# Three pairs of r tiles and one more gate pair as seven products of quarters, with linear attention's outputs parked in DRAM

## The chip, the cores and the metric

The kernel runs on one core of one Trainium2 chip. Its time is the device time of one execution in microseconds; a kernel's time is the median of its runs. Beside them stands one execution that the hardware profiler recorded. All lines L... are lines of the kernel before.

## What is computed

One decoder layer runs over 560 tokens: 512 prompt tokens, 32 sample tokens (8 sequences of 4) and 16 meta tokens. Two half-step FFNs stand around a mixer with two branches, gated linear attention and stick-breaking attention. The mixer is where the change is:

```python
u = rms_norm(h, mix_pre_g)
proj = u @ w_in                       # q_a, k_a, v_a, gk, r_a, q_b, k_b, v_b, gate_a, gate_b
o_a, s_new = gla_branch(q_a, k_a, v_a, g, s0, lead)
o_a = rms_norm(o_a, gla_norm_g).reshape(B, L, V_GLA) * jax.nn.silu(r_a)
o_b = sb_attend(q_b, keys, vals, sb_bias, q_off)      # keys of sample tokens: cache pages by page_table
m = jax.nn.sigmoid(gate_a) * (o_a @ w_o_gla) + jax.nn.sigmoid(gate_b) * (o_b @ w_o_sb)
h = h + rms_norm(m @ w_out, mix_post_g)
```

All is float32. The model width is 1024, so r_a, gate_a, gate_b, o_a and o_b are 1024 wide each.

## The kernel before

**Layout and products.** Activations lie transposed: 128 features on the partitions, the tokens along the row. A tile of a product is 128 output features by all tokens, over eight blocks of 128 input features. Each float32 operand is split into two float32r parts: `hi`, a cast, and `lo`, the difference. A product is hi·hi + hi·lo + lo·hi, three matmuls. TensorE is PE in the profile, VectorE DVE, ScalarE ACT, GpSimd POOL, SyncE SP.

**Two kinds of tiles.** A plain tile ("R" in the lists, `tile_steps`, L674 to L687) does the eight blocks for two column halves of 280 and 264 tokens: eight steps of six matmuls. A pair of tiles ("S", `seven_steps`, L998 to L1032) takes two weight tiles as a 2 by 2 matrix of quarters and the activations as another, and makes the four result quarters from seven quarter products instead of eight, by Strassen's scheme in Winograd's form. It is 14 steps of six matmuls of 272 columns. It needs sums of weight quarters (`weight_sums`), sums of activation quarters (`usum`, s1 to s4) and sums of products. Its four accumulators a, d, b, c take all four PSUM buffers of the tag `acc`; `copied` and `add` take the products out.

**Steps set the order.** PE, VectorE, ScalarE and GpSimd run in the program's own order. The program counts steps: after each one `step()` runs what `later(n, f)` put n steps ahead, and then what `then` or `when` set for that step. So each engine's queue is written out by hand; an instruction that waits holds up all that stands behind it on its engine. SP, which issues the plain DMAs, is in order too, and runs ahead of the steps as far as its own waits let it.

**Stages.** FFN 1 (16 of its 22 hidden tiles as pairs of gate and up), its down product, the values, then linear attention by four heads (`Head`), whose outputs `oa[head, e]`, eight tiles of 544 tokens, stay in SBUF until the r tiles use them. Meanwhile the sums of quarters of u are made (`whole_u`, `u_sums`) and stored to `sums_dram`. Then eight passes for pairs of stick-breaking heads (`Pair`), 24 steps each: queries, keys and values of this pair, with the attention of the pair before in between. A ninth pass finishes the last pair; its 24 steps are the r tiles 0, 1 and 2 (`gate_r`).

**The mixer's list.** `MIXER` names the tiles that follow: r3 to r7, o0 to o7 (`out_a`, o_a @ w_o_gla), a0 and a1 (`gate_a`), then the pairs b0, a2 and b2 (`gate_pair`), the plain p0 and p1 (o_b @ w_o_sb), and so on. Of the sixteen gate tiles a0 and a1 are plain; the other fourteen are seven pairs, named by their first tile. The sums of u come back at steps 80 to 104 (`SUMS_BACK`) and are split into hi and lo 8 and 10 steps later. A plain r tile is done as follows: ScalarE takes sigmoids from the accumulators, VectorE multiplies by the accumulators and by `oa`, and `split` makes the parts `oas` that the o tiles read.

**Weights.** `st.todo` is the list of weight blocks; three blocks can be in flight (tag `raw`). `st.fetch` issues the next one on SP and waits until its buffer is free. `weights_at` lays out a pair's weight work around its first step n: sums at n - 10 to n - 8, parts b1 at n - 6 and n - 5, t at n - 2 and n - 1, b2 at n and n + 1, t4 at n + 4 and n + 6.

**The sample tokens' cache.** `ask` gathers four pages of keys or values by indirect DMA on the POOL queue (L2069) into rooms from `ring`, a list that each user refills when it is done. `use_keys` turns them (L2118), `sample_products` (L2132) and `sample_values` (L2218) multiply. All this is tied to step numbers of the ninth pass and of the mixer.

**Rooms.** `Arena` holds SBUF tiles: 25 rooms of six units, a unit being 280 columns. A request takes neighbouring units of a room that holds the same type, or of an empty one; among those that fit it takes the one given back longest ago. A writer of a room waits until the last reader of what lay there is done.

Of the kernel before, what the change touches and what calls it, by code (L numbers as in the profile page):

```python
# [1 line left out]

# [47 lines left out]
UNITS = 150  # L50


class Arena:
# [4 lines left out]
    CHUNK = 6  # L58

    def __init__(self, pool, n):  # L60
        self.pool, self.clock, self.made = pool, 0, 0
        self.freed = [[0] * self.CHUNK for _ in range(n // self.CHUNK)]
        self.tile = [None] * len(self.freed)
        self.held = {}
        self.keep = 0

    def take(self, width, dt=F32, tight=False):
# [3 lines left out]
        for c, free in enumerate(self.freed):  # L71
            empty = None not in free
            if not empty and self.tile[c].dtype != dt:
                continue
            for s in range(self.CHUNK - k + 1):
# [6 lines left out]
                key = (empty and empties <= self.keep, waste, tight and sum(x is not None for x in free), alone, since)  # L82
# [4 lines left out]
        if None not in self.freed[c] and (self.tile[c] is None or self.tile[c].dtype != dt):  # L87
            self.made += 1
            self.tile[c] = self.pool.tile([P, self.CHUNK * self.UNIT], dt, tag=f"room{c}", name=f"room{c}_{self.made}")
# [32 lines left out]
def hybrid_step(  # L122
# [15 lines left out]
    arena = Arena(cp, UNITS)  # L138
# [103 lines left out]
    ob_dram = dp.tile([8, P, NP], F32, name="ob_dram")  # L242
    sums_dram = dp.tile([4, 2, P, NP + NS], F32, name="sums_dram")
# [86 lines left out]
    class Head:  # L330
# [246 lines left out]
        def out(self, e):  # L577
# [867 lines left out]
    st.todo += [(win, 0, KD, C_RA + P * n, P, False) for n in range(8)]  # L1445
# [4 lines left out]

    for kind, what, n in MIXER[5:]:
        w, c = {"a": (win, C_GA), "b": (win, C_GB), "o": (w_o_gla[0], 0), "p": (w_o_sb[0], 0)}[what]
# [612 lines left out]
    ring = []  # L2065

    def page(src, i, c):
        t = ring.pop(0)
# [43 lines left out]
    def sample_keys(b, q, kp, kT):  # L2112
# [8 lines left out]
        if q:  # L2121
            ring.extend((kp[b, 0], kp[b, 1]))
# [88 lines left out]
    def sample_values(c, b0, vp, oz):  # L2211
# [8 lines left out]
        ring.extend(vp.values())  # L2220
# [62 lines left out]

    def gate_r(n):

        acc = yield from tile_steps(um, W1)
        sg, o = take(NW), oa[n // 2, n % 2]
# [16 lines left out]
    def gate_a(n):  # L2304
        acc = yield from tile_steps(um, W1)
        sg = take(NW)

        def sig():
            for h in range(2):
                S.activation(sg[:, h * HW : h * HW + W2[h]], acc[h][:, : W2[h]], AF.Sigmoid)  # L2310

        def by():
            tt(m1[n], sg, m1[n], ALU.mult)
# [388 lines left out]
```

## Time and profile before

| | |
|---|---|
| median of 3 runs | 1506.97 us (1506.46 to 1508.04) |
| the profiled execution | 1508.72 us, span 1507.0 us |
| granted clock | 0.999 |
| matmul records | 11941 |
| DMA | 180.40 MB, mean 120 GB/s |
| r tiles 0 to 7 | about 802 to 874 us of the span |
| o tiles | about 874 to 936 us |
| gate and p tiles | about 937 to 1068 us |

A row of a stretch gives, for each engine, its busy time and its number of instructions there, then the granted clock, the busy share of the DMA engines and what they moved. A row of a group of instructions gives line, engine, operation, output and inputs with their shapes, the count, then the busy time in us and the mean duration in ns, and behind the second bar the engine's idle time just before them with what ended it. A row of the timeline gives start and duration in us, and in brackets the idle time of the engine before it. The helper `tt` puts all VectorE operations of two tensors on L153, so those are told apart by tiles and shapes.

### The profile page before, as it was taken

What the parts mean: (1) busy time and instruction counts of PE and PEld (TensorE: products, weight loads), DVE (VectorE), ACT (ScalarE), POOL (GpSimd) and SP (SyncE); (2) the same over time, 40 slices, a digit from 0 to 9 for tenths busy, and PEclk for the clock granted to TensorE, in tenths of its full rate; (3) what the DMA queues carried; (4) which work ended last, traced back from release to release, by engine and by line L of the source; (5) the groups of instructions that cost most, each with busy time, mean ns of one, the idle gap of its engine ahead of it and who ended that gap; (6) DMA issues with size and microseconds to landing.
All of it is one profiled execution on the core that took longest, in us unless ns stands there. A gap on an engine that the chain in (4) does not pass through costs nothing.

```text
span 1507.0 us, 29698 instructions
## 1 busy us (share of the span) xinstructions
PE 1494.2 (99%) x11941; PEld 1442.1 (96%) x11941; DVE 1090.0 (72%) x1939; ACT 771.5 (51%) x1422; POOL 149.3 (10%) x216
## 2 busy tenths in 40 slices
PE   9999999999999999999999999999999999999998
PEld 8999999999999889999888899999999999999998
DVE  5888888853787866877776534977567898888544
ACT  6545454533655556565555343634564555455334
POOL 2000000000000011123324551000000000000000
PEclk9999999999999999999999999999999999999999
DMA  8123333336565473335555568335532233333352
GB/s 250 55 86 99 99 98 97 88 101 195 147 160 148 122 112 85 91 82 118 131 105 139 169 204 192 105 96 144 152 103 79 85 111 99 99 99 89 86 168 98
DMA packets 276458, 180.40 MB, mean 120 GB/s; under 512 B 10154, under 2 KB 260736, under 8 KB 276320
## 3 DMA queue, kind: packets, MB, share of 16 engines
q1 hardware_dynamic: 270864, 161.64, 40.6%
q0 software_dynamic: 5440, 16.85, 3.2%
q8 instruction: 94, 1.54, 0.4%
q14 instruction: 44, 0.36, 0.1%
q10 hardware_dynamic: 16, 0.00, 0.0%
HBM read 155.72 MB, written 22.74 MB: 118 GB/s over the span
## 4 chain that ended last, share of the span: by engine, by line
PE 94%; DVE 2%; DMA 2%; ACT 1%; issue 0%; DVEq 0%; SPq 0%; ACTq 0%
PE acc L682 8%; PE acc L1248 8%; PE acc L1249 8%; PE acc L685 8%; PE acc L683 8%; PE acc L1250 8%; PE acc L695 7%; PE acc L698 7%; PE acc L696 7%; PE acc L1191 2%; PE acc L1188 2%; PE acc L1189 2%; PE acc L1028 1%; PE acc L1029 1%; PE acc L1030 1%; PE ps L2023 1%
## 5 line engine op out<-in xcount | busy, mean ns | idle before, releaser
L153 DVE TENSOR_TENSOR lo<-raw,hi 128x1024 fp32r<-128x1024 f32 (+1 forms) x213 | 254.9, 1197 | 125.9 <-ACT hi L661 102.5
L153 DVE TENSOR_TENSOR room<-room,room 128x544 f32<-128x544 f32 (+17 forms) x413 | 259.0, 649 | 81.4 <-ACT room L740 15.0
L682 PE MATMUL acc<-room,hi 128*128 128x280 f32 (+1 forms) x928 | 271.2, 309 | 0.2 <-DVE room L156 0.2
L1249 PE MATMUL acc<-room,hi 128*128 128x280 f32 (+1 forms) x896 | 259.3, 289 | 0.0
L1248 PE MATMUL acc<-room,hi 128*128 128x280 f32 (+1 forms) x896 | 259.3, 289 | 0.0
L1250 PE MATMUL acc<-room,lo 128*128 128x280 f32 (+1 forms) x896 | 259.1, 289 | 0.0
L683 PE MATMUL acc<-room,hi 128*128 128x280 f32 (+1 forms) x928 | 250.3, 289 | 0.1
L685 PE MATMUL acc<-room,lo 128*128 128x280 f32 (+1 forms) x928 | 192.8, 289 | 0.0
L682 PEld LDWEIGHTS acc<-room,hi 128*128 128x128 f32 x928 | 174.7, 188 | 13.1 <-issue 11.0
L683 PEld LDWEIGHTS acc<-room,hi 128*128 128x128 f32 x928 | 175.0, 189 | 2.8 <-issue 1.9
L1248 PEld LDWEIGHTS acc<-room,hi 128*128 128x128 f32 x896 | 168.6, 188 | 0.0
L1250 PEld LDWEIGHTS acc<-room,lo 128*128 128x128 f32 x896 | 168.6, 188 | 0.0
L1249 PEld LDWEIGHTS acc<-room,hi 128*128 128x128 f32 x896 | 168.4, 188 | 0.0
L959 ACT CAST hi<-raw 128x1024 fp32r<-128x1024 f32 x92 | 96.4, 1052 | 133.1 <-PE acc L1249 48.8
L661 ACT CAST hi<-raw 128x1024 fp32r<-128x1024 f32 (+1 forms) x121 | 122.7, 1015 | 72.0 <-DMA raw<-in_ffn_w_down_dram 18.6
L685 PEld LDWEIGHTS acc<-room,lo 128*128 128x128 f32 x928 | 145.0, 188 | 0.0
L695 PE MATMUL acc<-room,hi 128*128 128x280 f32 (+2 forms) x498 | 143.7, 296 | 0.9 <-ACT hi L661 0.9
L696 PE MATMUL acc<-room,hi 128*128 128x280 f32 (+2 forms) x498 | 141.5, 292 | 0.0
L698 PE MATMUL acc<-room,lo 128*128 128x280 f32 (+2 forms) x498 | 128.4, 292 | 0.7 <-DVE lo L153 0.7
L959 ACT CAST hi<-room 128x1024 fp32r<-128x1024 f32 x84 | 70.2, 836 | 80.8 <-PE acc L1249 60.3
L695 PE MATMUL acc<-room,room 128*128 128x280 f32 (+3 forms) x366 | 107.8, 295 | 0.0
L153 DVE TENSOR_TENSOR lo<-room,hi 128x1024 fp32r<-128x1024 f32 x84 | 80.2, 955 | 36.7 <-ACT hi L959 36.5
(406 smaller groups left out, 3299.5 us busy)
## 6 DMA issues: line engine op xcount, KB each, us to landing
raw<-in_w_in_dram SPq DMA_DIRECT2D x49, 512.0 KB
raw<-in_ffn_w_down_dram SPq DMA_DIRECT2D x40, 448.0 KB
raw<-in_ffn_w_gate_dram SPq DMA_DIRECT2D x64, 256.0 KB
raw<-in_ffn_w_up_dram SPq DMA_DIRECT2D x64, 256.0 KB
out_dram<-room SPq DMA_DIRECT2D x36, 256.0 KB
raw<-in_ffn_w_down_dram SPq DMA_DIRECT2D x14, 512.0 KB
raw<-in_w_in_dram SPq DMA_DIRECT2D x28, 256.0 KB
h_dram<-room SPq DMA_DIRECT2D x24, 280.0 KB
```

The source lines that it names most:

```text
L153: (eng or V).tensor_tensor(out=out, in0=a, in1=b, op=op)
L661: S.copy(h_, src)
L682: T.matmul(acc[h][:, : wid[h]], hi[k], a[h][0], start=(k == 0), stop=False)
L683: T.matmul(acc[h][:, : wid[h]], hi[k], a[h][1], start=False, stop=False)
L685: T.matmul(acc[h][:, : wid[h]], lo[k], a[h][0], start=False, stop=(k == KD - 1))
L695: T.matmul(acc[h][:nw, : wid[h]], wh, a[h][0], start=(k == 0), stop=False)
L696: T.matmul(acc[h][:nw, : wid[h]], wh, a[h][1], start=False, stop=False)
L698: T.matmul(acc[h][:nw, : wid[h]], wl, a[h][0], start=False, stop=(k == kt - 1))
L959: S.copy(hi[:, :kt], src)
L1248: T.matmul(x[:, :QW], hi, act[k][0], start=(first and k == 0), stop=False, skip_group_check=True)
L1249: T.matmul(x[:, :QW], hi, act[k][1], start=False, stop=False, skip_group_check=True)
L1250: T.matmul(x[:, :QW], lo, act[k][0], start=False, stop=(k == 3), skip_group_check=True)
```

## The change

- r2 and r3, r4 and r5, r6 and r7 become three pairs (`r_pair`), a0 and a1 become one (`gate_pair`). `gate_a` goes. The ninth pass now runs the first 24 steps of the mixer's own chain: r0, r1 and eight steps of r2's pair. Step 0 stays at the end of that pass, so r0 has step -24.
- In `r_pair` VectorE makes the four result quarters in two tiles `t`, ScalarE their sigmoids, VectorE multiplies `oa` by both, and `split` follows.
- The sums of u come back at steps -31 to -19 and are split 5 to 8 steps later.
- Each head's two outputs `oa` are stored to `oa_dram` and their rooms given back; `oa_back` reads them again, for a plain tile at its start, for a pair at its sixth step.
- The second column halves of u's first four tiles are given back before r2 (`halved`).
- Pages get a room at each ask instead of one from `ring`, and the asks have a spacing of their own: steps 7, 15, 23, 31, 39, 63, 71, 79 and 87 of the mixer, before 7 to 63 by eights and 87.
- `Arena` has 14 rooms of six units and 33 of two; a request of up to two units takes a short room if any fits.
- The splits of o_b for the p tiles start 6 steps after b0's beginning, before 2.

```diff
-SUMS_BACK = (80, 88, 96, 104)
-MIXER = [("R", "r", n) for n in range(3, 8)]
-MIXER += [("R", "o", n) for n in range(8)] + [("R", "a", 0), ("R", "a", 1), ("S", "b", 0), ("S", "a", 2), ("S", "b", 2), ("R", "p", 0), ("R", "p", 1)]
+SUMS_BACK = (-31, -27, -23, -19)
+MIXER = [("R", "r", 0), ("R", "r", 1), ("S", "r", 2), ("S", "r", 4), ("S", "r", 6)]
+MIXER += [("R", "o", n) for n in range(8)] + [("S", "a", 0), ("S", "b", 0), ("S", "a", 2), ("S", "b", 2), ("R", "p", 0), ("R", "p", 1)]
...
-    CHUNK = 6
+    LONG, SHORT = 6, 2
...
-        self.freed = [[0] * self.CHUNK for _ in range(n // self.CHUNK)]
+        self.freed = [[0] * self.LONG for _ in range(n)] + [[0] * self.SHORT for _ in range((UNITS - n * self.LONG) // self.SHORT)]
...
-                key = (empty and empties <= self.keep, waste, tight and sum(x is not None for x in free), alone, since)
+                key = (k <= self.SHORT < len(free), empty and empties <= self.keep, waste, tight and sum(x is not None for x in free), alone, since)
...
                 give(*self.on)
+                for e in range(2):
+                    later(1, lambda e=e: nc.sync.dma_start(oa_dram[2 * hd + e], oa[hd, e]))
+                    later(6, lambda e=e: give(oa.pop((hd, e))))
...
-        t = ring.pop(0)
+        t = take(512)
...
-        ring.extend(vp.values())
+        give(*vp.values())
...
+    def oa_back(n):
+        o = take(NW)
+        nc.sync.dma_start(o, oa_dram[n])
+        return o
...
     def gate_r(n):
+        o = oa_back(n)
         acc = yield from tile_steps(um, W1)
-        sg, o = take(NW), oa[n // 2, n % 2]
+        sg = take(NW)
...
+    def r_pair(n):
+        o, t, sg, outs = {}, {}, {}, {}
+        q0, q1 = slice(0, QW), slice(QW, NW)
+        def load():
+            for i in range(2):
+                o[i] = oa_back(n + i)
+        def second():
+            t[1] = take(NW)
+            outs.update(c12=t[1][:, q0], c22=t[1][:, q1])
+        def first():
+            t[0] = take(NW)
+            outs.update(c11=lambda a: S.copy(t[0][:, q0], a), c21=t[0][:, q1])
+        def by_t(i):
+            sg[i] = take(NW)
+            S.activation(sg[i], t[i], AF.Sigmoid)
+            tt(o[i], o[i], t[i], ALU.mult)
+        def by_sg(i):
+            tt(o[i], o[i], sg[i], ALU.mult)
+            give(t[i], sg[i])
+            split(oas, n + i, o[i], oap)
+        for d, f in ((6, load), (10, second), (11, first), (14, lambda: by_t(1)), (15, lambda: by_sg(1)), (16, lambda: by_t(0)),
+                     (17, lambda: by_sg(0))):
+            later(d, f)
+        yield from seven_steps(("r", n), usum, QW, outs)
...
-        for k in (i, i + 4):
-            for h in range(2):
+            for h in range(1 if k < 4 else 2):
...
+        starts, n = {}, -24
+        for i in range(4):
+            when(SUMS_BACK[i], sums_back, i)
+            for m in range(2):
+                when(SUMS_BACK[i] + 5 + m, sums_hi, i, m)
+                when(SUMS_BACK[i] + 7 + m, sums_lo, i, m)
...
-            for n in FE:
+            for n in FE if now else ():
...
-            for main in (now.queries, now.keys, now.values) if now else (lambda i=i: gate_r(i) for i in range(3)):
+            for main in (now.queries, now.keys, now.values) if now else (lambda: islice(mixer, 24),):
...
-            when(8 * i + 7, ask)
+        for i in range(3, 12):
+            when(8 * i - 17 if i < 8 else 8 * i - 1, ask)
...
-            when(starts["b", 0] + 2 + 4 * i, lambda i=i: split(obs, i, ob[i], obp))
+            when(starts["b", 0] + 6 + 4 * i, lambda i=i: split(obs, i, ob[i], obp))
```

More of the change, by code (lines that the diff above doesn't have):

```diff
@@ L2121, in sample_keys @@
         if q:
-            ring.extend((kp[b, 0], kp[b, 1]))
+            give(kp[b, 0], kp[b, 1])
     def sample_products(c, b0, q, kT, z):
@@ L2445, in hybrid_step @@
                 then(SUM[1], last.meta_summed)
-            if pr == 4:
-                ring += [take(512) for _ in range(4)]
             if pr > 4:
@@ L2568, in hybrid_step @@
         when(starts["p", 6] + 2, h_back)
[L2569 removed]
         n = 0
[L2571 to L2581 removed]
+        for _ in mixer:
+            n += 1
+            step()
+            for f, args in mixer_at.pop(n, ()):
+                f(*args)
+        assert not mixer_at, sorted(mixer_at)
         hT_room = hT_room_
```

107 lines of the change are left out of this document (48 added, 59 removed).

## The prediction

> **What bounds the kernel now.** First the page: busy time of the engines (part 1) and the chain of waits (part 4).
>
> ```profile
> PE 1494.2 (99%) x11941; PEld 1442.1 (96%) x11941; DVE 1090.0 (72%) x1939; ACT 771.5 (51%) x1422; POOL 149.3 (10%) x216
> ...
> PE 94%; DVE 2%; DMA 2%; ACT 1%; issue 0%; DVEq 0%; SPq 0%; ACTq 0%
> ```
>
> PE is busy 1494.2 of 1507.0 us and makes up 94% of the chain. Whatever takes matmuls away shortens the run, as long as nothing else begins to hold PE up. So the second view is the list of PE's own waits over the whole run, of which the two in the part that changes are these (us in total, times, longest):
>
> ```profile
> PE ps L2218 <- issue: 2.7, 5, 0.8
> ...
> PE acc L1028 <- DVE room L153: 0.3, 1, 0.3
> ```
>
> The 2.7 us lie in the sample-value matmuls and wait for nothing that the profile shows; the 0.3 us are a quarter-product tile waiting for VectorE. Third, busy time by stretch: the first four r tiles with the rest of the last attention pair, the other four r tiles, the three gate pairs that run back to back, and a piece of the second FFN, which is all seven-product tiles.
>
> ```profile
> core 0: us, PE busy (x) PEld busy (x) DVE busy (x) ACT busy (x) POOL busy (x), PEclk, DMA share, GB/s
> 802.00:839.00 37.00, 36.97 (x357) 33.53 (x356) 25.73 (x73) 17.46 (x37) 18.39 (x21) 1.00 0.63 161
> 839.00:874.00 35.00, 33.72 (x340) 31.22 (x339) 14.70 (x22) 13.36 (x24) 18.19 (x17) 1.00 0.52 169
> 949.00:982.00 33.00, 32.69 (x259) 32.25 (x258) 31.06 (x53) 20.57 (x35) 0.00 (x0) 1.00 0.35 94
> ...
> 1190.00:1300.00 110.00, 110.00 (x883) 110.00 (x882) 98.28 (x149) 55.70 (x86) 0.00 (x0) 1.00 0.33 97
> ```
>
> Two things are to be seen. The granted clock is 1.00 throughout. And seven-product tiles live with a VectorE that is busy 31.06 of 33.00 us (94%) or 98.28 of 110.00 us (89%), with PE idle 0.31 us in the first and not at all in the second. VectorE is the engine next to the limit.
>
> **The change part by part.** *What PE is spared.* Six r tiles and the two gate tiles a0 and a1 become four pairs of seven products. Two plain tiles are 16 steps of six matmuls, a pair 14 steps of six. The price of plain steps is in PE's timeline from the start of p0 to the start of the pair after p1, the price of a pair in ScalarE's timeline of the FFN's sixteen pairs of the same width (272 columns):
>
> ```profile
> 982.20 0.29 PE L682 MATMUL acc<-room,hi 128*128 128x280 f32 x1
> ...
> 994.27 0.29 PE L1028 MATMUL acc<-room,hi 128*128 128x272 f32 x1
> ```
>
> ```profile
> 1203.61 0.40 ACT L1240 ACTIVATE room<-acc 128x272 f32<-128x272 f32 x1 [0.54 <-PE acc L1250]
> ...
> 1360.91 0.40 ACT L1240 ACTIVATE room<-acc 128x272 f32<-128x272 f32 x1 [0.55 <-PE acc L1250]
> ```
>
> 16 plain steps take 994.27 - 982.20 = 12.07 us, 0.754 us each. Fifteen pair periods are 157.30 us, so a pair takes 10.49 us. Each replacement saves 1.58 us, four save 6.3 us. No other PE work is added or removed: the sample matmuls keep their step numbers, only the eight o tiles and all that follows come six steps sooner relative to them.
>
> *What VectorE gets.* The rows of the gate stretch give the price of each operation of a pair (mean ns behind the comma):
>
> ```profile
> L153 DVE TENSOR_TENSOR lo<-raw,hi 128x1024 fp32r<-128x1024 f32 x6 | 7.3, 1217 | 0.0
> L153 DVE TENSOR_TENSOR room<-room,room 128x544 fp32r<-128x544 f32 x8 | 5.7, 718 | 0.0
> L153 DVE TENSOR_TENSOR room<-room,acc 128x272 f32<-128x272 f32 x11 | 4.6, 432 | 0.4 <-PE acc L1030 0.4
> ...
> L153 DVE TENSOR_TENSOR room<-raw,raw 128x512 f32<-128x512 f32 x4 | 2.8, 690 | 0.4 <-DMA raw<-in_w_in_dram 0.4
> L153 DVE TENSOR_TENSOR room<-room,room 128x544 f32<-128x544 f32 x3 | 2.1, 715 | 0.0
> L153 DVE TENSOR_TENSOR lo<-room,hi 128x512 fp32r<-128x512 f32 x3 | 2.1, 685 | 0.0
> ```
>
> An r pair costs four weight sums (4 x 0.69), low parts of the weights (3 x 1.22 + 0.69), five sums of products (5 x 0.43), four multiplications of 544 columns (4 x 0.72) and two low parts of results (2 x 0.72): 13.6 us. What it replaces is in the stretch of the first r tiles, three of each:
>
> ```profile
> L153 DVE TENSOR_TENSOR lo<-raw,hi 128x1024 fp32r<-128x1024 f32 x3 | 3.7, 1225 | 7.5 <-ACT hi L661 7.5
> L153 DVE TENSOR_TENSOR room<-room,room 128x544 f32<-128x544 f32 x3 | 2.2, 749 | 0.1
> L153 DVE TENSOR_TENSOR room<-room,room 128x544 fp32r<-128x544 f32 x3 | 2.1, 712 | 0.0
> ...
> L153 DVE TENSOR_TENSOR room<-acc,room 128x280 f32<-128x280 f32 x3 | 1.3, 439 | 0.0
> L153 DVE TENSOR_TENSOR room<-acc,room 128x264 f32<-128x264 f32 x3 | 1.3, 418 | 0.0
> ```
>
> That is 10.6 us for three tiles, 3.5 us a tile, 7.1 us for two. A pair adds 6.5 us of VectorE and takes 1.58 us of PE away.
>
> The load falls unevenly. Take the 32 steps that now last the 37.0 us from 802 to 839. Work other than r tiles is 25.7 - 10.6 = 15.1 us. Then come r0 and r1 without their weights (6.9 x 2/3 = 4.6), the low parts of the sums of u, which the change moves here from the o tiles (seven of the eight, 7 x 0.72 = 5.0), the pair r2 but for its last three operations (11.4) and most of r4's weights (four sums, three low parts: 6.4). Together 42.5 us by durations. Successive rows overlap by some 0.08 us, so about 38.5 us of queue in 37.0 us. In the 26 steps after that it is easy: 1.5 of other work (14.7 in the second row less four r tiles at 3.3, the 3.5 without the overlap), 2.2 left of r2, 7.1 of r4, 8.8 of r6 with its weights, 1.2 for o0's weights: 20.8 us in 26 x 35.0/32 = 28 us. So VectorE runs behind by a growing amount until the end of r2 and recovers in r4. I put the lag at its worst at 3 to 5 us: the overload of 1.5 us, and the idle time that it cannot use because its input is not there.
>
> Who waits for that? VectorE is in order, so behind each late operation stand the evacuations of PSUM. The summing of the last attention pair needs a transposed tile from VectorE:
>
> ```profile
> 819.74 0.56 DVE L2010 COPY room<-ps 128x384 f32<-128x384 f32 x1 [0.88 <-PE ps L2032]
> ...
> 821.09 2.38 PE L2023 MATMUL ps<-room,room 128*64 128x512 f32 x16
> ```
>
> The copy ends at 820.3, PE starts at 821.1 and needs it only for the last third of the 2.38 us, a margin of about 2 us; up to there the added queue is 8.2 us of sums and weights less 2.3 us of weights removed, 5.9 us against 4.4 us of idle VectorE, so the copy comes 1.5 us later and still fits. Next, r4's second product reuses the accumulator that r2's c12 reads; c12 is issued three steps ahead of it, some 3.5 us, against a lag of 3 to 5 us. That is the tight place. The weights of a pair have five steps, 5.8 us at 37.0/32 = 1.16 us a step, and hold. The nearest measured price for such a miss is the one in the gate pairs:
>
> ```profile
> 970.05 0.40 PE L1028 MATMUL acc<-room,hi 128*128 128x272 f32 x1 [0.28 <-DVE room L153]
> ```
>
> So an added wait of VectorE costs from 0.28 us (one such miss) to 5.5 us (the whole of 42.5 - 37.0 handed to PE); I take 0.9 us for the r pairs, near the low end, since 94% cost 0.31 us in all. For the gate pair a0, which joins b0, a2 and b2 to a run of four, I take 0.3 us more, one more miss. Nothing here can be a gain beyond the 2.7 us of L2218, which has no shown cause.
>
> *ScalarE.* It is busy 17.46 of 37.00 us; in the gate stretch the same pairs with the same splits use 20.57 of 33.00 us. It has room, but it is in order too, and the first cast of the sums of u waits for a DMA.
>
> *The sums of u and the outputs o, to and from DRAM.* The reads of the sums (8 x 272 KB) now start 5 steps ahead of their cast instead of 8, 5.8 us. SP issues the last pair behind the store of the keys, where it now issues a 512 KB weight block:
>
> ```profile
> 807.52 0.46 SPq L186 DMA_DIRECT2D raw<-in_w_in_dram  x1
> ...
> 814.84 1.06 ACT L661 CAST hi<-raw 128x1024 fp32r<-128x1024 f32 x1
> ```
>
> That block was cast 7.3 us after its issue without a wait for it, beside the same page gathers, so 544 KB need at most about 7.7 us, and the wait of ScalarE is between 0 and 1.9 us. Behind it are two PSUM copies whose buffers PE wants again four steps (4.6 us) later. I put 0.2 us of it on PE. The Trainium skill ("DMA: Bandwidth & Descriptors", Specifications; Anatomy of one DMA; Queues, rings and completion order) gives some 2 us fixed, 358 GB/s from HBM, and turns between the queues; an estimate by that page with half the rate beside the gathers is 2.0 + 3.1 = 5.1 us, no wait, and the sum would be 0.2 us smaller.
>
> The eight outputs o go out once and come back eight or more steps ahead of their use (6.0 us at the least, 9.3 us at this stretch's pace): 4.5 MB more on 180 MB. Cost on PE zero; the cover is that lead, and without it each late tile would cost the two VectorE multiplications behind it a wait, not PE. Page rooms taken per ask instead of from a ring let POOL start gathers sooner; the page is used 18 steps after the ask as before. Zero. Moving SP's fetches out of the last pass and into the pairs' own schedule keeps three blocks in flight. Zero.
>
> *Rooms of two lengths* change where every tile of the kernel lies. The trace shows no operation for it. Its two sides: nothing, or a wait at every pair (a rival below); I take 0.2 us because a room of two units is never shared by more than two tiles.
>
> **The sum.** -6.3 + 0.9 + 0.3 + 0.2 + 0.2 = -4.7 us. The profiled execution took 1508.7 us with a span of 1507.0 us, so its own sum is 1504.0 us; against the median of 1506.97 us it is **1502.3 us**. A measurement of this kernel tells 0.2%, 3.0 us, from no change.
>
> **The rivals.**
> 1. *Forecast*, 1500.5 to 1503.9 us: PE's saving less one to three microseconds of waits. 0.51.
> 2. *All of the saving, or a little more*: VectorE's lag stays within the leads, and the 2.7 us at L2218 shrink. For it: 89% in the FFN with PE never idle. Against: the 38.5 us in 37.0. 1506.97 - 6.3 = 1500.7 less up to 2.0: 1498.7 to 1500.5. 0.15.
> 3. *VectorE becomes the bound of the first r pairs.* For it: the sum above, and the tight accumulator. Against: the easy 26 steps behind. It hands PE 42.5 - 37.0 = 5.5 us in place of 0.9: 1506.9, or 1504 to 1510. 0.18.
> 4. *The short rooms.* A request of up to two units takes a short room even if it was given back a moment ago, while long ones lie idle. Then a writer waits for the last reader of that room: ScalarE, copying a product out of PSUM, would wait for VectorE's addition that lags. Place: all 32 pairs of the FFNs and the 11 of the mixer, 43. Price: 0.28 us each, the one miss shown, is 12.0 us: 1506.97 - 6.3 + 1.4 + 12.0 = 1514. It turns the saving of 4.9 into a loss from 4.9/43 = 0.11 us a pair. For it: 89% VectorE in the FFN leaves 1.1 us a pair. Against: readers are a step or more ahead of the next writer there, and PE has no wait at all in that stretch now. 0.13.
> 5. *Gathers held off by VectorE.* The rows:
>
> ```profile
> L2069 POOL DMA_INDIRECT room<-in_cache_k_dram,idx x32: 944/1139/1761, 680.3 to 866.3; - x32
> L2069 POOL DMA_INDIRECT room<-in_cache_v_dram,idx x32: 942/946/1954, 813.9 to 920.4; - x32
> ```
>
> A gather takes 0.94 us at least and up to 1.95 us. If all four of an ask take the latter, an ask lasts 4 x (1.95 + 0.3 between two) = 9.0 us, and with 7.3 us to land it needs 16.3 us; 18 bare steps are 13.6 us, 2.7 us short, and six asks make 16 us: about 1518. At the r stretch's 1.16 us a step the lead is 20.9 us and nothing is late, so 0.02. By the Trainium skill ("SBUF — State Buffer", Who interferes with whom) VectorE and GpSimd share a port pair as an exclusive lock, which speaks for this one; how much of the spread comes from it no row here tells.
> 6. *The change is not in the instructions*: the matmuls of the mixer's pairs would stay at 196 per line. 1507. 0.01.
>
> **Range and chances.** Faster by over 0.2% (below 1504.0): cases 1 and 2, 0.66. Within 0.2%: case 3 almost whole and case 6, 0.18. Slower: cases 4 and 5 and the tail of 3, 0.16. The range leaves out the lowest part of case 2 and most of cases 4 and 5: 1499.5 to 1509.0 us. The likeliest case's own range is 1500.5 to 1503.9.
>
> **What would show it.** Right: the mixer's pair lines go from 196 to 308 matmuls each, the plain tile line L682's 928 to 800; the time from r0's first matmul to the first o tile shrinks by 4.7 us less waits; PE's waits on VectorE or ScalarE in the r stretch add up to 0.3 to 2 us; VectorE's busy share over the first 32 steps is above 95%; the FFNs' pair period stays at 10.49 us. Wrong: a pair period in the FFN that is longer (case 4), PE waiting in the r pairs for 3 us or more (case 3), PE waiting at L2218 or L2118 for POOL's gathers (case 5), or ScalarE's casts of the sums of u standing on a DMA for longer than 2 us.

## The result, and the profile after

The changed kernel takes 1525.56 us (median of 4 runs, 1524.92 to 1529.18) against 1507.26 us on the same chip: 1.0126 times the time before, interval 1.0114 to 1.0138. The medians lie 18.3 us apart, by the ratio it is 19.0 us slower; 4.7 us faster had been forecast. Its profiled execution took 1524.99 us with a span of 1523.0 us.

The page, busy time and chain:

```profile
PE 1496.4 (98%) x11893; PEld 1440.6 (95%) x11893; DVE 1115.3 (73%) x1977; ACT 781.0 (51%) x1434; POOL 144.0 (9%) x216
...
PE 88%; DVE 6%; DMA 3%; issue 1%; ACT 1%; DVEq 0%; SPq 0%; ACTq 0%
```

There are 48 matmuls fewer, as the four pairs make them, and yet PE is busy 2.2 us longer, and its share of the chain falls from 94% to 88%. VectorE's share rises from 2% to 6%, DMA's from 2% to 3%. PE's idle time is 1523.0 - 1496.4 = 26.6 us, before it was 12.8: 13.8 us more. Busy longer with less to do: the granted clock is 0.995 on average, before 0.999. Added up in steps of 2 us, stretches at half clock take 6.3 us of PE's busy time here and took 1.7 us before.

The instructions are those that were promised (groups of PE, lines of the changed kernel):

```profile
L689 PE MATMUL acc<-room,hi 128*128 128x280 f32 (+1 forms) x800 | 236.1, 311 | 0.2 <-DVE room L159 0.2
...
L1035 PE MATMUL acc<-room,hi 128*128 128x272 f32 x308 | 91.5, 297 | 2.6 <-DVE room L156 2.6
```

Where is the time lost? The same operations of ScalarE, before and after, serve as milestones: the heads' first values, the sums of the eight attention passes, the o tiles.

```profile
L370 ACT ACTIVATE room<-ps,rcol x16: 448/474/490, 464.8 to 533.7; 128x256 f32<-128x256 f32 x16
...
L2041 ACT COPY room<-ps x8: 585/587/589, 613.1 to 825.3; 128x512 f32<-128x512 f32 x8
...
L2370 ACT COPY room<-acc x16: 383/390/393, 883.8 to 936.5; 128x280 f32<-128x280 f32 x8, 128x264 f32<-128x264 f32 x8
```

```profile
L374 ACT ACTIVATE room<-ps,rcol x16: 467/476/493, 462.5 to 538.4; 128x256 f32<-128x256 f32 x16
...
L2047 ACT COPY room<-ps x8: 586/587/588, 620.8 to 835.4; 128x512 f32<-128x512 f32 x8
...
L2397 ACT COPY room<-acc x16: 381/390/398, 894.4 to 952.7; 128x280 f32<-128x280 f32 x8, 128x264 f32<-128x264 f32 x8
...
L1247 ACT ACTIVATE room<-acc x16: 397/398/399, 1219.6 to 1377.1; 128x272 f32<-128x272 f32 x16
```

The heads start 2.3 us earlier than before (462.5 against 464.8; 1.7 us of this is a stretch at half clock from about 346 to 349 in the execution before, which the changed kernel's does not have) and the first pass ends 7.7 us later (620.8 against 613.1). **So 10.0 us are lost in the four linear-attention heads, a part of the kernel whose products the change does not touch.** The last pass's sum, which lies among the r tiles already, comes 10.1 us later, and the first o tile 10.6 us, although the three r pairs have saved 4.7 us by then: from the first pass to there 10.6 - 7.7 + 4.7 = 7.6 us are lost. The o tiles add 5.6 us (16.2 at their last copy). At the last pair of the second FFN it is 16.2 us still (1377.1 against 1360.9), so the gate tiles have lost the 1.6 us that they saved. Sixteen FFN pairs from 1219.6 to 1377.1 are still 10.50 us each.

Busy time by stretch, before and after: the heads, and 40 us of the r tiles.

```profile
465.00:585.00 120.00, 119.77 (x879) 106.07 (x878) 86.82 (x193) 68.75 (x182) 12.93 (x31) 1.00 0.57 121
...
815.00:855.00 40.00, 38.75 (x401) 34.82 (x399) 22.21 (x58) 16.09 (x33) 18.11 (x21) 1.00 0.58 184
```

```profile
465.00:585.00 120.00, 113.70 (x801) 99.16 (x800) 81.48 (x181) 59.92 (x156) 12.82 (x31) 0.97 0.59 133
...
815.00:855.00 40.00, 35.91 (x374) 31.38 (x373) 38.92 (x89) 21.81 (x42) 19.40 (x20) 1.00 0.64 183
```

In the heads PE was idle for 0.2 us and is idle for 6.3 us now, at a clock of 0.97. No engine is fuller than before there. In the r tiles VectorE is busy 38.92 of 40 us, before 22.21. These are two different troubles.

**One wait of the heads, followed back.** Three lines of the timeline, VectorE, ScalarE and PE (start, duration, and in brackets the idle time and what ended it):

```profile
535.89 0.69 DVE L156 TENSOR_TENSOR room<-room,dec 128x512 f32<-128x512 f32 x1 [3.96 <-DMA out_dram<-room]
...
537.32 1.57 ACT L374 ACTIVATE room<-ps,rcol 128x256 f32<-128x256 f32 x4 [3.89 <-DVE room L156]
...
538.21 1.01 PE L464 MATMUL ps<-room,room 128*128 128x128 f32 x3 [2.47 <-ACT room L374]
```

VectorE wants to write a tile of keys into a room and must wait 3.96 us until a store has read it out. ScalarE waits for VectorE, PE for ScalarE. Which store? The source line L536, `sample_state_out`, which stores a head's sample states and gives the room back in the next statement, `give(s0)`:

```profile
L536 SPq DMA_DIRECT2D out_dram<-room x16: 372/373/977, 497.5 to 589.6; - x16
its engine sat idle before it (us, times) until:
who waited for it (us, times):
  ACT room L585: 6.0, 1
  POOL room L1823: 5.8, 1
  DVE room L156: 5.5, 2
```

With long rooms only, a request took, among the places that fit, the one given back longest ago. Now two-unit requests go to short rooms first, and the next taker comes while the store is still under way.

**The wait is paid for twice, in this execution.** Busy time in steps of 2 us from 537 on (the ninth figure is the granted clock, behind the count of POOL):

```profile
537.00:539.00 2.00, 0.79 (x3) 0.79 (x4) 0.30 (x1) 1.68 (x5) 0.00 (x0) 0.68 0.45 147
539.00:541.00 2.00, 2.00 (x14) 1.78 (x13) 1.56 (x4) 0.99 (x4) 0.20 (x1) 0.50 0.65 180
541.00:543.00 2.00, 2.00 (x11) 1.82 (x10) 0.70 (x1) 0.59 (x1) 0.64 (x1) 0.50 0.66 237
543.00:545.00 2.00, 2.00 (x11) 1.86 (x10) 0.09 (x1) 1.04 (x3) 0.52 (x1) 0.62 0.86 59
545.00:547.00 2.00, 2.00 (x26) 1.44 (x25) 1.96 (x5) 0.44 (x2) 0.50 (x2) 1.00 1.02 60
```

The four steps up to 545 lose 0.64, 1.00, 1.00 and 0.76 us, together 3.4 us, which is 6.8 us at half clock after 2.47 us of idle PE: more than the wait itself. The Trainium skill ("TensorE: Matmul & The Clock Gate", What's actually happening) says that the clock is either full or half, and is set by activity in windows of 3.4 us; the 0.50 agrees, and so does the length, twice 3.4 us here. Its advice to avoid idle gaps of more than about 3 us (Why this matters for your kernels) is too generous here: 2.47 us were enough.

But the clock does not follow from the length of the wait. In another profiled execution of the same kernel (run e6 below) PE waits 2.27 us at the same place, and the heads run at full clock. From their first values to the first pass's sum it takes 155.3 us, the execution above 158.3, the kernel before 148.3: 7.0 us are lost there without the clock, 10.0 with it. The heads in e6:

```profile
465.00:585.00 120.00, 113.90 (x825) 99.55 (x824) 82.26 (x184) 62.97 (x164) 13.92 (x31) 1.00 0.60 135
```

PE's waits over the whole run, the longer ones:

```profile
PE ps L2222 <- issue: 4.6, 9, 1.0
PE ps L2193 <- DVE room L156: 2.6, 2, 2.1
PE acc L1035 <- DVE room L156: 2.6, 2, 2.2
PE ps L464 <- ACT room L374: 2.5, 1, 2.5
PE ps L486 <- DVE room L159: 1.8, 2, 1.5
PE ps L527 <- DVE room L159: 1.5, 1, 1.5
PE ps L2013 <- ACT room L2016: 1.4, 1, 1.4
```

L464, L486 and L527 are in the heads; L2013 (turning the last pass's weights) and L2193 (turning the samples' weights) in the r tiles; L1035 in the run of gate pairs; L2222 at the samples' values, 1.7 us of it among the r pairs and 3.0 us among the o tiles.

The sum: 13.8 us of idle time and 4.6 us of clock more than before, less 6.3 us of products, is 12.1 of the 16.0 us of span. The other 3.9 us stay open.

### The profile page after: what moved, and what is told of

The parts are those of the page before. It is cut to its first block, busy times and chain, and to the rows that moved or that the text cites. A ratio compares the mean times of both kernels' runs of the same rounds, so it can differ in the third digit from the quotient of the medians.

```text
span 1523.0 us, 29778 instructions
## 1 busy us (share of the span) xinstructions
PE 1496.4 (98%) x11893; PEld 1440.6 (95%) x11893; DVE 1115.3 (73%) x1977; ACT 781.0 (51%) x1434; POOL 144.0 (9%) x216
## 4 chain that ended last, share of the span: by engine, by line
PE 88%; DVE 6%; DMA 3%; issue 1%; ACT 1%; DVEq 0%; SPq 0%; ACTq 0%
PE acc L1255 7%; PE acc L1257 7%; PE acc L1256 7%; PE acc L702 7%; PE acc L705 7%; PE acc L703 7%; PE acc L689 6%; PE acc L692 6%; PE acc L690 6%; DVE room L156 3%; PE acc L1035 2%; PE acc L1036 2%; PE acc L1037 2%; PE acc L1198 1%; PE acc L1195 1%
## 5 line engine op out<-in xcount | busy, mean ns | idle before, releaser
L156 DVE TENSOR_TENSOR room<-room,room 128x544 fp32r<-128x544 f32 (+18 forms) x425 | 259.4, 633 | 55.2 <-ACT room L768 9.6
L1255 PE MATMUL acc<-room,hi 128*128 128x280 f32 (+1 forms) x896 | 259.7, 290 | 0.0
L1257 PE MATMUL acc<-room,lo 128*128 128x280 f32 (+1 forms) x896 | 259.3, 289 | 0.0
L1256 PE MATMUL acc<-room,hi 128*128 128x280 f32 (+1 forms) x896 | 259.2, 289 | 0.0
L689 PE MATMUL acc<-room,hi 128*128 128x280 f32 (+1 forms) x800 | 236.1, 311 | 0.2 <-DVE room L159 0.2
L690 PE MATMUL acc<-room,hi 128*128 128x280 f32 (+1 forms) x800 | 217.3, 290 | 0.0
L966 ACT CAST hi<-raw 128x1024 fp32r<-128x1024 f32 x100 | 104.8, 1052 | 142.5 <-PE acc L1256 75.0
L1256 PEld LDWEIGHTS acc<-room,hi 128*128 128x128 f32 x896 | 168.9, 189 | 0.0
L1257 PEld LDWEIGHTS acc<-room,lo 128*128 128x128 f32 x896 | 168.9, 188 | 0.0
L1255 PEld LDWEIGHTS acc<-room,hi 128*128 128x128 f32 x896 | 168.6, 188 | 0.0
L692 PE MATMUL acc<-room,lo 128*128 128x280 f32 (+1 forms) x800 | 167.3, 290 | 0.1
L689 PEld LDWEIGHTS acc<-room,hi 128*128 128x128 f32 x800 | 151.6, 189 | 12.2 <-issue 10.2
L690 PEld LDWEIGHTS acc<-room,hi 128*128 128x128 f32 x800 | 151.8, 190 | 2.5 <-issue 1.7
L668 ACT CAST hi<-raw 128x1024 fp32r<-128x1024 f32 (+1 forms) x113 | 114.3, 1012 | 69.3 <-DMA raw<-in_ffn_w_down_dram 17.1
L692 PEld LDWEIGHTS acc<-room,lo 128*128 128x128 f32 x800 | 125.7, 189 | 0.5 <-issue 0.5
L966 ACT CAST hi<-room 128x1024 fp32r<-128x1024 f32 x92 | 76.9, 836 | 86.0 <-PE acc L1256 58.2
L156 DVE TENSOR_TENSOR lo<-room,hi 128x1024 fp32r<-128x1024 f32 x92 | 87.9, 956 | 38.1 <-ACT hi L966 37.9
```

The costliest lines, as they stand in the source:

```text
L156: (eng or V).tensor_tensor(out=out, in0=a, in1=b, op=op)
L668: S.copy(h_, src)
L689: T.matmul(acc[h][:, : wid[h]], hi[k], a[h][0], start=(k == 0), stop=False)
L690: T.matmul(acc[h][:, : wid[h]], hi[k], a[h][1], start=False, stop=False)
L692: T.matmul(acc[h][:, : wid[h]], lo[k], a[h][0], start=False, stop=(k == KD - 1))
L966: S.copy(hi[:, :kt], src)
```

## The experiments

The theory after this: the heads' 10 us come from the two lengths of rooms (A), the r tiles' from a full VectorE (D), and the gate pairs' from something still to be found. Fifteen kernels were run in four groups, each group on one chip with its own runs of the kernel before. That took 1502.62, 1506.69, 1502.15 and 1506.44 us in the four, a difference of 0.3% that returns below. Line numbers shift by a few from kernel to kernel.

### The heads: rooms or parked outputs

`e2` puts the two-length rooms into the kernel before, `e3` the parking of o; `e4` and `e5` alter the changed kernel.

```diff
# e2: the class Arena of the changed kernel, UNITS, LONGS = 150, 14
# e3, in Head.out and gate_r of the kernel before
+                    later(1, lambda e=e: nc.sync.dma_start(oa_dram[2 * hd + e], oa[hd, e]))
+                    later(6, lambda e=e: give(oa.pop((hd, e))))
+        o = take(NW)
+        nc.sync.dma_start(o, oa_dram[n])
# e4; fresh is 40 while the heads are laid out, else 0
-                key = (k <= self.SHORT < len(free), empty ...
+                key = (self.clock - max(f) < self.fresh, k <= self.SHORT < len(free), empty ...
# e5, in sample_state_out
-            give(s0)
+            later(8, lambda: give(s0))
```

> The kernel before, with one part of the change alone: rooms of two lengths (14 of six units, the others of two, short ones taken first). Theory A (a short room is taken again soon after it is given back, so the four linear attention heads, 465 to 585 us, wait for stores that still read it): the heads lose most of the 10 us that they lost in the changed kernel, time 1514 to 1519, with waits for rooms that a store ends in that stretch. Rival B (the parked outputs' stores and early returns cost it): nothing, 1506.5 to 1508.5. Rival C (only the r pairs' VectorE work costs anything, and the clock after it): 1507 as well, and no new PE waits in the heads.

> The kernel before, with one other part alone: linear attention's outputs are stored to DRAM from the heads, their rooms given back six steps later, and fetched again at each r tile. Theory A: 1506.5 to 1509, PE idle in the heads under 1 us. Rival B: 1514 to 1519, with PE idle of some 6 us in the heads.

> The changed kernel, with one rule more while the heads are laid out: a room given back less than 40 returns ago is taken only if there is no other. Theory A: the heads' loss goes, time 1515 to 1518 against 1525.6, PE idle in the heads from 6.3 us to under 1.5 us, clock there back to 1.00. Rival B: the stores are the same, so the time stays at 1525 and the idle time with it.

> The changed kernel; the four rooms of each head's sample states are given back eight steps after their store is issued instead of at once. Theory A as I state it (the wait is for the store in flight, most of all the sample states'): 1517 to 1521, since the longest waits of ScalarE (6.0 us) and GpSimd (5.8 us) in the heads lose their releaser. If it is quick reuse as such, whatever reads the room last: 1524 to 1526. Rival B: 1525.

Measured, as ratios to the kernel before: e2 1.0084 (1.0068 to 1.0101), e3 0.9995 (0.9986 to 1.0005), e4 1.0029 (1.0017 to 1.0040), e5 1.0053 (1.0037 to 1.0070). The heads in their windows, e2, e3, e4, e5 in this order:

```profile
465.00:585.00 120.00, 114.35 (x820) 100.41 (x819) 82.47 (x185) 62.50 (x166) 11.58 (x28) 0.99 0.56 121
```

```profile
465.00:585.00 120.00, 119.77 (x878) 106.08 (x877) 86.50 (x193) 68.72 (x181) 12.79 (x31) 1.00 0.62 141
```

```profile
465.00:585.00 120.00, 119.83 (x881) 106.63 (x880) 87.13 (x194) 69.57 (x181) 12.85 (x31) 1.00 0.60 137
```

```profile
465.00:585.00 120.00, 116.77 (x854) 103.38 (x854) 85.25 (x191) 65.84 (x174) 12.46 (x31) 1.00 0.60 138
```

PE's idle time in the heads is 5.7 us with the rooms alone and 0.2 us with the parking alone. The rooms alone cost 12.6 us by the ratio (10 to 15 by its interval; the two profiled executions, spans of 1511.2 us in e2 and 1500.5 us in e3, are 10.7 us apart); the parking costs nothing that can be measured. Theory A holds, B is refuted, and so is C. In e2 the loss reaches past the heads into the first attention pass, by the same mechanism: ScalarE waits for a store that still reads its room, and PE then waits 2.5 us for ScalarE.

```profile
613.99 0.48 ACT L2012 COPY room<-ps 128x384 f32<-128x384 f32 x1 [5.00 <-DMA out_dram<-room]
```

Letting rooms rest while the heads are laid out (e4) brings the idle time there from 6.3 to 0.2 us. The changed kernel was not run in this group, so its ratio, 1.0126, cannot be set beside e4's 1.0029; the milestones can. From the heads' first values to the first pass's sum e4 takes 148.0 us, as long as the kernel before (148.3). Keeping only the rooms of the sample states eight steps longer (e5) takes away every wait for `out_dram` in the heads and half of the idle time (3.2 us left, before the products at L486 and L527, which wait for VectorE); from milestone to milestone it takes 151.5 us, against 155.3 in e6, both at full clock there. So the store in flight is about half of the mechanism. The rest goes when rooms rest, so it is quick reuse too, behind other readers; which readers was not followed.

What the pairs cost without the heads' trouble is the difference of e4 and e3, one group, neither with a stall that the view lists. Of 3.7 us of span, 7.4 us are idle time and 1.4 us clock, less 6.3 us of products; that accounts for 2.5 us. The waits of the r tiles and of the gate pairs are dearer than the products saved.

### The r tiles and the gates

```diff
# e6: the changed kernel again. e7, e8, e9 on top of e4:
# e7
+MIXER = [("R", "r", n) for n in range(8)]
# e8
+MIXER = [("R", "r", n) for n in range(4)] + [("S", "r", 4), ("S", "r", 6)]
+SUMS_BACK = (-23, -19, -15, -11)
# e9, for pages alone: fresh is 30
+        t = take(512, rest=30)
```

> The changed kernel itself, beside the others on one chip. All theories: 1.011 to 1.014 times the kernel before if the loss is the kernel's own. If the PE stalls with no releaser in the trace (4.6 us in the changed kernel's first profile, 2.7 us in that of before) belong to that execution and not to the change, they are gone here and the ratio is 1.008 to 1.011.

> The heads-rested kernel with all eight r tiles as plain tiles again (a0 stays a pair). Theory D (with the three r pairs VectorE is full, 54.9 of the 60 us from 795 to 855, and the last attention pair's and the samples' turns wait behind it, 4.4 us of PE idle, 6 to 7 with the clock after it): 4.7 us of products come back and 6 to 7 go, so 1 to 3 us below the heads-rested kernel, and PE idle in 803 to 875 under 0.5 us. Rival E (the waits in that stretch come from the rooms, not from the pairs): 4 to 5 us above the heads-rested kernel, idle unchanged.

> The heads-rested kernel with r0 to r3 plain and two pairs, r4 and r6, so that the first pair starts eight steps into the stretch that the last attention pair has left, the sums fetched eight steps later. Theory D: 1.6 us of products come back, most of the 4.4 us of idle goes: 3 to 6 us below the heads-rested kernel, 0 to 3 below the kernel before. Rival F (a pair of r tiles costs its stalls wherever it lies, since its adds and splits are as many): 0 to 2 us above the heads-rested kernel.

> The heads-rested kernel; a page's place, too, is one given back at least 30 returns ago if there is one. Theory D says that a0's wait (3.8 us at 951 to 956) is for VectorE, which stands for weights that DMA brings late (2.4 us at once) since the last gathers, held back for page rooms still in use (GpSimd waits up to 14 us), are on the queues then (DMA share 0.92 from 930 to 940): gathers go earlier, the wait shrinks below 1 us, 3 to 6 us below the heads-rested kernel. Rival G (the weights are late for another reason, their own place in the raw ring): the same time within 1.5 us.

Measured: e6 1.0122 (1.0105 to 1.0139), e7 1.0051 (1.0034 to 1.0067), e8 1.0044 (1.0029 to 1.0058), e9 1.0053 (1.0037 to 1.0070). These ratios cannot be set beside e4's 1.0029, since e4 is not in this group: here every kernel shows PE stalls without a releaser among the gathers, in the group of e4 none does. The changed kernel's loss repeats (e6), again with 4.6 us of such stalls; e8, forecast at the kernel before or up to 3 us below it, is 0.4% above. PE's waits from 803 to 937 in e6 and e4 (the kernel before has there only the 2.7 us at L2218):

```profile
PE ps L2222 <- issue: 4.6, 8, 1.0
PE ps L2193 <- DVE room L156: 2.6, 2, 2.1
PE ps L2013 <- ACT room L2016: 1.4, 1, 1.4
PE ps L1980 <- ACT room L1906: 0.3, 1, 0.3
```

```profile
PE ps L2196 <- DVE room L157: 2.2, 1, 2.2
PE ps L2016 <- ACT room L2019: 1.0, 1, 1.0
PE ps L2196 <- ACT room L2179: 0.5, 1, 0.5
```

The waits for an engine are alike in both groups, those for "issue" are not. So I judge by the waits. With plain r tiles (e7) VectorE falls from 38.79 to 27.92 of 40 us, and PE's waits in that stretch, apart from "issue", from 4.3 us (e4, 585 to 937) to 1.5 us; the waits before L2016 and L2196 go from 1.0 and 2.7 us to nothing and 0.2 us. The 40 us are, e4 and e7:

```profile
805.00:845.00 40.00, 36.26 (x364) 31.77 (x366) 38.79 (x89) 22.18 (x43) 18.70 (x20) 1.00 0.61 177
```

```profile
805.00:845.00 40.00, 37.64 (x376) 31.95 (x374) 27.92 (x72) 18.58 (x39) 20.68 (x22) 1.00 0.82 209
```

Theory D holds for these waits: the pairs' sums and splits hold up VectorE, and PE stands for the turns, not for the r pairs' own accumulators. E, that the rooms make them, falls. With two later pairs (e8) 2.1 us behind VectorE are left at L693 and L2196: less, but not gone. Rested page rooms (e9) left the wait among the gate pairs at 3.3 us: G, not the late gathers.

### The wait among the gate pairs

The expectations call this wait a0's. Counting PE's matmuls from the start of a0 puts it one pair later: it is the seventh product of b0, the second of the four pairs. That product adds onto accumulator c, and VectorE must first have taken the fourth product out of it. VectorE's sum and PE's next matmul in e4:

```profile
955.23 0.44 DVE L157 TENSOR_TENSOR room<-room,acc 128x272 f32<-128x272 f32 x1
955.73 0.59 PE L1036 MATMUL acc<-room,hi 128*128 128x272 f32 x1 [3.82 <-DVE room L157]
```

So here PE does stand for a pair's own accumulator, whose sum comes late because of what lies ahead of it in VectorE's queue.

```diff
# e10, on top of e4 (e13 has + 10 + i in the first line, e16 + 6 + i and plain r tiles)
-            when(starts["a", 0] + 2 + i, ob_back, i)
+            when(starts["a", 0] + 2 + 2 * i, ob_back, i)
+            when(n + 5 + 4 * i, sample_out, 2 + i)        # copies of one ob, not of four
# e11: e10 with the two r pairs of e8. e12: e10, and in sums_lo
+        tt(lo[:, :NW], ..., ALU.subtract, G if i < 2 else V)
# e14: e13, and the samples' first weights from step 21 instead of 17
+                then(21, lambda: todo.extend([n, f] for n, f in w0.pieces(1)))
# e15: e14 with the two r pairs of e8
```

> The heads-rested kernel; around the first pair of gate tiles, attention's outputs are fetched back every second step instead of every step, and the sixteen small copies of the samples' outputs into them are spread, two ahead of each split, instead of eight at a time. Theory H (a0's wait, 3.8 us at 951 to 956, comes from the two pairs' preparations meeting these fetches, 2.1 MB issued from 925 to 936 with b0's weights on the same queues, and these copies, 3.2 us of VectorE): the wait falls under 1.5 us, time 3 to 5 us below the heads-rested kernel (1.0029 times before) where the chip has no stalls without a releaser, ratio 0.999 to 1.001. Rival: the pair's own sums and splits are too many for VectorE there; wait stays over 3 us, ratio 1.002 to 1.006.

> The same with r0 to r3 plain and two pairs, r4 and r6. Theories D and H together: 1.6 us of products back, waits of the r stretch (3.7 us of idle with three pairs) under 2 us: 1 to 3 us below the kernel of the run before, ratio 0.997 to 1.000. If the r pairs' waits are as large later (F): ratio 0.5 to 1.5 us above the run before.

> The kernel of the first of these three runs, with half of the low parts of the sums of u (4 of 8, first ones) made on GpSimd instead of VectorE ahead of the r pairs. Theory D: VectorE loses 3 us of its queue before 810, so PE's waits for the turns of the samples and of the last pair in 800 to 850 fall by 1.5 to 3 us, time 1.5 to 4 us lower. Rival: GpSimd's own queue stands for page rooms (5 to 6 us at a time) or its operation is slow, the sums come late and PE waits at the first r pair: same time or up to 5 us more.

Measured: e10 1.0029 (1.0018 to 1.0041), e11 1.0023 (1.0013 to 1.0033), e12 1.0033 (1.0022 to 1.0045). My theories' forecasts were met in none of the three; the ratios of e10 and e12 lie where their rivals put them. The wait among the gate pairs went from 3.8 to 2.7 us in e10 and the ratio stayed at e4's. With the pairs later (e11) 2.2 us at L2196 and 1.3 at L693 are left. In e12 GpSimd made half of the low parts and the waits at L2196 stayed at 2.7 us: VectorE is busy 8.40 instead of 9.79 us from 805 to 815, and 9.79 and 9.36 us in both kernels in the two ten-microsecond stretches behind. What it saves around 810 does not reach the turns 30 us later.

In e10 VectorE still waited for weights, which come behind the fetch of seven outputs issued from 931.7 to 938.1; in e13 all of that fetch but the first output goes out after them. VectorE's lines, e10 and e13:

```profile
950.05 0.69 DVE L157 TENSOR_TENSOR room<-raw,raw 128x512 f32<-128x512 f32 x1 [2.90 <-DMA raw<-in_w_in_dram]
```

```profile
945.51 0.69 DVE L157 TENSOR_TENSOR room<-raw,raw 128x512 f32<-128x512 f32 x1 [0.64 <-DMA raw<-in_w_in_dram]
```

> The heads-rested kernel with the samples' copies spread as in the earlier run, and attention's outputs fetched back from the tenth step after a0's start instead of the second. Theory J (a0's wait is made by b0's weights landing 10 us after they are issued, since 2.1 MB of outputs are issued just before them, and VectorE standing 2.9 us for them): VectorE's wait for raw weights near 947 falls under 0.5 us and PE's at a0 under 0.7 us (2.7 before); time 2.5 to 4 us less, ratio 0.9995 to 1.0015 on a chip without unexplained stalls. Rival K (VectorE is simply full there): PE waits 2 us or more as before, ratio unchanged at 1.003.

> The kernel of the run before with the samples' weights of the first half made four steps (2.9 us of products) later. Theory D: PE's two turns of them then find their operands made, the 2.7 us of waits (2.2 for VectorE, 0.5 for ScalarE) fall under 1 us, and the granted clock after it (0.67 in the 5 us from 835) stays at 1.00: 2.5 to 4 us less than the run before. Rival: VectorE is the bound of the stretch, the wait turns up at the next thing PE needs from it (an adder of the pair, an r tile's parts): less than 1 us gained.

> Both moves with r0 to r3 plain and two pairs, r4 and r6. If D and J hold: 4.7 us of products saved against the kernel before and under 3 us lost, ratio 0.997 to 0.9995. If the waits move on to other places: 1.000 to 1.003.

> The heads-rested kernel with all r tiles plain, a0 a pair, and the outputs fetched back from the sixth step after a0's start: only a0's 1.6 us saved. J: PE's wait at a0 (2.5 us with plain r and the early fetch) under 0.7 us, ratio 0.998 to 1.000. K: still over 2 us, ratio 1.001 to 1.004.

Measured: e13 1.0062 (1.0045 to 1.0079), e14 1.0046 (1.0027 to 1.0064), e15 1.0021 (1.0012 to 1.0031), e16 1.0059 (1.0042 to 1.0076), all with "issue" stalls again (4.3 us in e13). The ratios forecast under J came in none of e13, e15 and e16; e15's lies where the waits move on. e14 is 3.4 us below e13 by the medians, as D forecast, though not by D's account, as will be seen. In e14 the rooms of the first half's queries go back before its later products read them, so part of the samples' attention computes on other numbers; the instructions are the same. e15 gives these rooms back just as early, so neither is a version to build on. PE's waits at the gate pairs, e10, e13 and e16 (from the timeline):

```profile
955.34 0.39 PE L1036 MATMUL acc<-room,hi 128*128 128x272 f32 x1 [2.18 <-DVE room L157]
968.01 0.39 PE L1036 MATMUL acc<-room,hi 128*128 128x272 f32 x1 [0.35 <-DVE room L157]
```

```profile
975.85 0.40 PE L1036 MATMUL acc<-room,hi 128*128 128x272 f32 x1 [1.39 <-DVE room L157]
```

```profile
963.38 0.39 PE L1036 MATMUL acc<-room,hi 128*128 128x272 f32 x1 [1.14 <-DVE room L157]
976.75 0.40 PE L1036 MATMUL acc<-room,hi 128*128 128x272 f32 x1 [2.57 <-DVE room L157]
```

J is half right. In e10 the late weights made the wait at b0's seventh product: with them in time it is gone in e13. (In the changed kernel itself VectorE waits only 0.35 us for weights there, and PE 2.2 us; VectorE's queue holds 3.2 us of the samples' copies.) But the wait at the same product of the next pair, a2, grows from 0.35 us to 1.4 us, and to 2.6 us in e16, where no DMA holds VectorE up: its queue is packed there with the next pair's weight sums and the splits of the outputs (K). e14's later samples' weights shrink the wait at L2196 from 2.7 to 1.6 us, and 1.7 us turn up at L2240, which reads what VectorE copies last of them and whose own step was not moved. In these runs a wait behind a full VectorE moved on rather than went away.

No version beat the kernel before. The nearest are e3, which has no new pair (0.9995, no difference), and e15 (1.0021).

## Why the prediction was wrong

**The step that failed first is "Rooms of two lengths ... I take 0.2 us".** The rooms alone cost 12.6 us by the ratio of e2, 10.7 us between profiled spans. The reason given, that a short room "is never shared by more than two tiles", looks at neighbours; what counts is how soon a room is taken again and who still reads it. Rival 4 had the mechanism, a writer that waits for the last reader of a room just given back, and a price of 12.0 us that is near the 12.6 by accident. It had the wrong place, the FFN pairs, whose period stayed at 10.50 us, and the wrong reader, VectorE instead of DMA stores, which make about half of the loss (e5). The prediction looked at stages that the pairs touch, and not at those where rooms are given back right after a store.

**"The granted clock is 1.00 throughout"** is right for the stretches shown there and was taken for the whole run and for the changed kernel. The profiled execution before itself has 3.4 us at half clock, from about 346 to 349. Every wait was priced at its own length, and the changed kernel loses 6.3 us of busy time to the clock, 1.7 us before.

**The r pairs: 0.9 us taken, 4.3 us of waits measured** (L2193 2.6, L2013 1.4, L1980 0.3), near the upper bound of 5.5 us that rival 3 used. The load was about right: 38.5 us of queue in 37.0 us were forecast, 38.92 of 40 us are seen. The place was wrong: the accumulator of c12 has no wait there. PE waits for what else stands in VectorE's queue, the turns of the samples' and the last pass's weights. The margin of the first such copy had been worked out and its later siblings not. The choice of the low end, "since 94% cost 0.31 us in all", set a stretch with nothing foreign in the queue beside one full of it.

**The gate pair a0: 0.3 us taken, 2.3 us measured** (2.6 us of waits in the run of gate pairs, 0.3 before), 1.6 to 4.3 us in its variants. The kind of miss was the right one, the seventh product of the second pair, which cost 0.28 us before; now it costs 2.2 us. The samples' copies and the fetch of attention's outputs, which now meet two pairs' preparations, were not in the working.

**Right:** PE's saving as instructions (308 and 800 matmuls per line); the FFN untouched; the parked outputs at zero (e3); the sums of u, for which neither ScalarE nor VectorE waits on a DMA from 780 to 830, so that even the 0.2 us was not needed. For "Page rooms: zero" there is this: the o tiles lost 5.6 us in the changed kernel, with 3.0 us of "issue" stalls (0.8 before) and 3.4 us at half clock, but in e4, which has the same page rooms and no such stalls, they take 53.1 us from first to last copy against 52.2 us in e3. Stalls of this kind stand in all kernels of two groups, plain r tiles or not, and in none of the other two, and their cause was not found.

## What to carry to other kernels

A change of where tiles lie has no instruction in the profile, but it decides who waits for whom: list every buffer that is given back while a store still reads it, and ask how soon the next writer comes. An engine that is 90% busy gives slack only if the others wait for nothing else in its queue; look for all that stands there, not for the new operations alone. And a wait of PE can cost more than twice its length when the clock falls to half behind it (2.47 us of wait and 3.4 us of clock here); whether it falls differed from one execution of the same kernel to the next.

## What the hardware showed unexpectedly

Idle time of 2.47 us on PE was followed by some 6.8 us at half clock; in e6, the same kernel, 2.27 us at the same place were followed by none. A wait of 2.06 us that ended at 845.9 left the clock at 1.00, and the same wait in e6 was followed by 3.4 us at half. Two waits of 0.90 and 0.73 us at 343 and 344 in the kernel before were followed by 3.4 us at half; waits of 0.8 and 0.7 us at the same place in e13 by none. In e4 a wait of 3.8 us that ended at 955.7 was followed by a mean of 0.66 from 955 to 960. In each of these cases the stretch at half lasted about 3.4 us, or twice that, and cost 1.7 or 3.4 us.

The kernel before took 1502.2 and 1502.6 us in two groups and 1506.4 to 1507.3 us elsewhere, and the traces of all kernels tell these apart: 2.7 to 4.6 us of PE stalls without a releaser between 803 and 937 us, where pages are gathered, or none that the view lists. They cost more than the list says: from the last pass's sum to the first o tile the kernel before takes 58.5 us, 2.0 us of them idle, and e3, with the same products there, 53.9 us. In the changed kernel they end 0.71 to 0.73 us apart, or twice that (among the o tiles at 929.93, 931.38, 932.11, 932.83, 933.54 and 934.25).
